# A two-layer hybrid transformer step: the odd layer's attention in the pool of the DeltaNet's preparation

## Chip, cores and metric

The kernel runs on one core of a Trainium2 chip. The metric is the device time of one execution in microseconds (us). Engines are named as the profile does: PE is TensorE (PEld its weight load, PEq, SPq and the like the sequencers that issue for an engine), DVE is VectorE, ACT is ScalarE, POOL is GpSimd, and SP is the engine that issues most DMAs. Each engine runs its own queue of instructions in order.

## What is computed

One step of a trunk with two layers on 128 context tokens and 1024 latent tokens, 1024 features wide. Each layer has a mixing part and a convolutional feed-forward part. The odd layer, which the change touches, mixes in two ways side by side: windowed attention with a sink (mixer C, 8 query heads and 2 key heads of 64) and a gated DeltaNet in two directions (mixer D). Cut to what matters, with jax.numpy as jnp:

```
cq, ck, cv, dq, dk, dv, da, db, dz = split_cols(h @ w_in, OD_SIZES)
q = axial_rope(cq...)            # latent tokens only; x1*cos - x2*sin, x1*sin + x2*cos
k = axial_rope(ck...)
# window_attn: 128 queries against their own block, both neighbours, and 128 cached keys
s_loc = jnp.where(valid, einsum(qn, kn) * scale, -inf)
s_ctx = einsum(qn, ck_cache) * scale
p = softmax_sink(concatenate([s_loc, s_ctx]), sink)
o_c = einsum(p, [vn, cv_cache])
# delta_scan, 64 tokens a chunk: a unit lower triangular system for each chunk and head
m_mat = a_mat + eye(64)
sol = triangular_solve(m_mat, rhs)
out = concatenate([o_c, o_d]) @ w_out
```

The 128 context tokens attend to each other without a window and without rotation. The gates dz (z0 to z3 below) multiply the DeltaNet's output much later.

## The kernel before

All matrices are float32. A projection splits weights and activations into a high and a low part and sums three matmuls for each block of 128 features (`gemm8`, L156 to L158: high by high, high by low, low by high). One chunk of weights is 128 x 1024: SP loads it (L134), ACT casts the high part `whi` (L141), DVE subtracts it to get the low part `wlo` (L144). One projected chunk of 128 columns takes 72 matmuls, in three blocks of tokens with 24 each.

`odd_1` (L1258) prepares the DeltaNet in pool "md". For four pairs of heads p = 0 to 3, `prep(p)` builds the matrices and `side(p)` the next pair's projections, and `inv(p)` inverts the 32 x 32 blocks of the systems on DVE: two directions with 31 steps of two instructions, a product `syst` (L1455) and a subtraction into `sysN` (L1457). POOL's queue stores the result in `n_dram` (L1460). `weave(main, fill)` and `mix` put steps of one generator between the steps of another. `side(3)` projects chunk c5 (values) and c4 (keys) of mixer C beside inv(2). Then `tail()` projects the query chunks c0 to c3, one for each pair of query heads. ACT copies each out (`df`, L1469) and makes a second copy with 32-row pieces swapped (L1473, four copies for each piece of tokens). `rope` (L1502) turns keys and queries: POOL or DVE multiplies the swapped copy by sines (L1506), DVE the other by cosines (L1507) and adds (L1509), and the result goes to `c_dram`. inv(3) is mixed into this on DVE. The order of DVE and POOL is written by hand there.

Then the pool closes and `odd_2` (L1535) runs in a new one, "mc": it projects the gates z0 and z3 (`odd_gate`), loads keys, values and queries from `c_dram` again (`cf`, `qp`), splits keys into `ks` and `kl` (L537 to L539) and queries into `qs` (L530, L531), and runs 36 attention units: for each pair p one unit with the 128 context queries (128 keys) and eight with 128 latent queries (512 keys inside, 384 at the ends). A unit's scores (PE L551, L552) go through the maximum `mx` (DVE L607), the negated maximum `nm` (L615), the exponential (ACT L617), the reciprocal of the sum and the normalisation (DVE L629, L632), the transposition `ptr` (PE L641, copied to `pt` by ACT L643) and the product with the values `pvo` (PE L652). `out` splits its result into `hh` (ACT L1622, then DVE L1623). `attn` has three units in flight: a turn issues the scores and the maximum of unit u, the normalisation of u-1, the transposition of u-2 and the product of u-3. The queries of the next pair are split in pieces of 576 columns during the units n = 2 and later of the current one.

As filler between units, `merge(p, d)` joins the inverted 32-blocks to 64-blocks: DVE transposes `tv` into `dT` (L1577), and for each third of the chunks PE does a group of small matmuls (a "quad", L1583, 24 records in the trace), ACT copies `zs` (L1589), PE does a second quad, and DVE writes the negated result into `tv` (L1597, two instructions): twelve quads for a pair of heads. `tv` is cleared by POOL first (L1568). The filler gets 1.8 units of debt for each attention unit. The orders of PE and DVE are written by hand here.

Of the kernel before, what the change touches and what calls it, by code (L numbers as in the profile page):

```python
# [9 lines left out]
F32 = mybir.dt.float32  # L10
# [43 lines left out]
class Net:  # L54
    def __init__(self, ctx, tc, I, O, dbg=None):
# [13 lines left out]
        self.nsc, self.sci = 6, 0  # L69
# [529 lines left out]
    def attn_exp(self, mp, u):  # L599
# [4 lines left out]
        for i in range(2):  # L604
            t = mp.tile([128, 512], F32, name="sc", tag=f"sc{self.sci}", bufs=1)
# [28 lines left out]
    def attn_tr(self, mp, u):  # L634
# [3 lines left out]
        for i in range(2):  # L638
            pt = self.pmt("ptr")
            for j in range(nk // 128):  # L640
                nc.tensor.transpose(pt[:, j * 128:(j + 1) * 128], u["sc"][i][:, j * 128:(j + 1) * 128], self.ident)  # L641
            t = mp.tile([128, 512], F32, name="pt", tag="pt", bufs=4)
            nc.scalar.copy(t[:, :nk], pt[:, :nk])  # L643
            u["pt"].append(t)
# [587 lines left out]
    def conv_ev(self, mp, w, dst):  # L1232
# [3 lines left out]
        def ev(b, ps):  # L1236
            n = FB[b][1]
            m = n - 2
            t = mp.tile([128, 388], F32, name="u", tag="du", bufs=2)
# [18 lines left out]
    def odd_1(self, mp, zp):  # L1258
        nc, I = self.nc, self.I
        mm = nc.tensor.matmul  # L1260
        D = self.dr
        self.kq_dram = D.tile([128, 18, 4, 4, 64], F32, name="kq_dram")
# [5 lines left out]
        dcw = mp.tile([128, 12, 3], F32, name="dcw", tag="dcw", bufs=1)  # L1268
        nc.sync.dma_start(dcw, I["dcw"])
        tri = {}  # L1270
        for nm in ("le", "ge", "gt", "lt", "bd"):
            tri[nm] = mp.tile([128, 128], F32, name=f"tri{nm}", tag=f"tri{nm}", bufs=1)
            nc.sync.dma_start(tri[nm], I[f"tri_{nm}"])
        half = []
        for d in range(2):
            t_ = tri["le" if d == 0 else "ge"]
            h = mp.tile([128, 64], F32, name="th", tag=f"th{d}", bufs=1)
            nc.vector.tensor_tensor(out=h, in0=t_[:, 0:64], in1=t_[:, 64:128], op=ALU.add)
            half.append(h.unsqueeze(1).to_broadcast([128, 18, 64]))
        g = mp.tile([128, 18, 8], F32, name="dg", tag="dg", bufs=1)  # L1280
# [4 lines left out]
        def gates():  # L1285
# [10 lines left out]
            sel = mp.tile([128, 18, 2, 8], F32, name="dsel", tag="dsel", bufs=1)  # L1296
# [7 lines left out]
            dtb = mp.tile([128, 8], F32, name="dtb", tag="dtb", bufs=1)  # L1304
            alg = mp.tile([128, 8], F32, name="alg", tag="alg", bufs=1)
# [5 lines left out]
            ab = mp.tile([128, 18, 8], F32, name="dabs", tag="dabs", bufs=1)  # L1311
# [20 lines left out]
        def df():  # L1332
            return mp.tile([128, T], F32, name="df", tag="df", bufs=4)
# [12 lines left out]

        def prep(p):
# [4 lines left out]
            for d in range(2):  # L1352
                X = mp.tile([128, 18, 64], F32, name="X", tag=f"am{d}", bufs=1)
                gg = g[:, :, 4 * d + p:4 * d + p + 1].to_broadcast([128, 18, 64])
                nc.vector.tensor_tensor(out=X, in0=gg, in1=half[d], op=ALU.mult)
                es.append((X, mp.tile([128, 18, 64], F32, name="E", tag=f"E{d}", bufs=1)))
            for x, nm in enumerate("kq"):
                s2[nm] = mp.tile([128, T], F32, name="s2", tag=f"aq{x}", bufs=1)
# [24 lines left out]
            def tok(nm, dr):  # L1383
                tt = mp.tile([128, T], F32, name="tt", tag="tt", bufs=2).rearrange("p (c t) -> p c t", t=64)
# [17 lines left out]
            aq = [mp.tile([128, 18, 64], F32, name="aq", tag=f"aq{d}", bufs=1) for d in range(2)]  # L1402
            am = [mp.tile([128, 18, 64], F32, name="am", tag=f"am{d}", bufs=1) for d in range(2)]
# [23 lines left out]
        def inv(p):  # L1427

            sy = []
            for d in range(2):  # L1430
                M = mp.tile([72, 32, 32], F32, name="sysM", tag=f"sysM{d}", bufs=1)
                N = mp.tile([72, 32, 32], F32, name="sysN", tag=f"sysN{d}", bufs=1)
# [8 lines left out]
                sy.append((M, N, tmp))  # L1441
            yield 0.0
            for jj in range(31):
                for d in range(2):
# [14 lines left out]
            for d in range(2):  # L1459
                nc.gpsimd.dma_start(self.n_dram[d, p], sy[d][1])  # L1460

        def proj_c(i):

            f = df()
# [11 lines left out]
            Q["c", i], Q["w", i] = f, w  # L1476

        def side(p):
# [6 lines left out]
            else:  # L1485
                yield from proj_c(5)
                nc.sync.dma_start(self.c_dram[5], Q["c", 5])
# [5 lines left out]
        self.plan += [("wi1", x) for x in (5, 4, 0, 1, 2, 3, 18, 21)]  # L1493
# [4 lines left out]
        cs, sn = Q["ropec"], Q["ropes"]  # L1498
# [3 lines left out]
        def rope(i):  # L1502
            f, w = Q["c", i], Q["w", i]
            r = f[:, 128:]
            eng = nc.gpsimd if i != 3 else nc.vector
            eng.tensor_tensor(out=w, in0=w, in1=sn, op=ALU.mult)  # L1506
            nc.vector.tensor_tensor(out=r, in0=r, in1=cs, op=ALU.mult)  # L1507
            yield
            nc.vector.tensor_tensor(out=r, in0=r, in1=w, op=ALU.add)  # L1509
            (nc.sync if i != 3 else nc.gpsimd).dma_start(self.c_dram[i], f)  # L1510
            yield

        def tail():
            prev = 4
            for i in range(4):
                pr, rp = proj_c(i), rope(prev)
                for c in pr:
                    next(rp, None)
                    yield c
                prev = i  # L1520
            for _ in rope(prev):
                pass

        E = mybir.EngineType
        with self.tc.manual_schedule(engines={E.DVE, E.Pool}):
            t, iv = tail(), inv(3)
            next(t)
            next(iv)
            for _ in range(2):
                next(t)  # L1530
            for _ in self.mix(t, iv, 1, 4):
                pass


    def odd_2(self, mp, zp):  # L1535
        nc, I = self.nc, self.I

        z0 = self.odd_gate(zp, 0)
        next(z0)
        mm = nc.tensor.matmul  # L1540
        R2 = [slice(0, 64), slice(64, 128)]
        kf = mp.tile([128, T], F32, name="cf", tag="cf", bufs=2)
        nc.sync.dma_start(kf, self.c_dram[4])
        vf = mp.tile([128, T], F32, name="cf", tag="cf", bufs=2)
        nc.sync.dma_start(vf, self.c_dram[5])
        mk = mp.tile([128, 1280], F32, name="maskC", tag="maskC", bufs=1)
        nc.sync.dma_start(mk, I["maskC"])
        VAR = [(0, 512), (512, 384), (896, 384)]
        sk = mp.tile([128, 4, 2], F32, name="sink", tag="sink", bufs=1)
        nsk = mp.tile([128, 4, 2], F32, name="nsink", tag="nsink", bufs=1)  # L1550
        nc.sync.dma_start(sk.rearrange("p a b -> p (a b)"), I["sink"].to_broadcast([128, 8]))
        nc.vector.tensor_scalar(out=nsk, in0=sk, scalar1=-1.0, scalar2=None, op0=ALU.mult)
        ks = [mp.tile([128, 1280], F32R, name="ks", tag=f"cks{i}", bufs=1) for i in range(2)]
        kl = self.new_kl(mp, "ckl", 1)
        ck = mp.tile([128, 128], F32, name="ck", tag="cck", bufs=1)
        nc.sync.dma_start(ck, I["ckT"])
        vt = mp.tile([128, 10, 128], F32, name="vt", tag="cvt", bufs=1)
        nc.sync.dma_start(vt[:, 8, :], I["cvc"])
        for _ in z0:
            pass  # L1560
        z3 = self.odd_gate(zp, 3)
        for _ in z3:
            pass

        def merge(p, d):

            t = self.tv[:, 2 * p + d]
            nc.gpsimd.memset(t, 0.0)  # L1568
            for r in range(2):
                for k in range(2):  # L1570
                    s0 = 64 * r + 32 * k
# [856 lines left out]
```

## Time and profile before

| | us |
|---|---|
| median of three runs | 3364.06 (3362.83 to 3365.55) |
| profiled execution | 3366.79 |
| its span | 3365.0 |
| PE busy in the span | 3209.0 (95%) |
| DVE busy | 2053.2 (61%) |
| ACT busy | 1432.6 (43%) |
| POOL busy | 659.9 (20%) |
| chain of work that ended last: PE, DVE, ACT | 82%, 9%, 4% |

Times of the trace count from the span's start. A busy share is an average over very different stages, so the rows below are taken from the stage that the change touches, 1951 to 2242 us. Busy time of PE is that of its matmuls, of which each is shown with its modelled end, so neighbouring ones overlap; starts are the better measure. The granted clock (PEclk) is a share of full speed.

### The profile page before, as it was taken

Reading aid. Unit: us, or ns where it says so; the run is one execution under the profiler, and the core shown is the slowest. Engines: PE = TensorE matmul, PEld = TensorE weight load, DVE = VectorE, ACT = ScalarE, POOL = GpSimd, SP = SyncE. Lnnn points to the kernel's source line nnn. Section 1 sums busy time; section 2 is a strip of 40 time slices with the busy share of each in tenths; the row PEclk is TensorE's granted clock in tenths of the full one; section 3 lists DMA queues with packets and bytes.
Section 4 is the critical chain, followed back from the end, with each engine's and each line's share of the span. In section 5 each row is a group of like instructions: output and inputs, shape, how many; then the busy total and the mean of one; then the engine's idle time right before and its main releaser. Section 6 shows DMA issues by size and latency. Waiting matters only on the chain.

```text
span 3365.0 us, 58552 instructions
## 1 busy us (share of the span) xinstructions
PE 3209.0 (95%) x23071; PEld 3042.3 (90%) x23071; DVE 2053.2 (61%) x4323; ACT 1432.6 (43%) x3264; POOL 659.9 (20%) x829
## 2 busy tenths in 40 slices
PE   7999999899999999999899977989989999999997
PEld 4999988789999999999799877878889999999997
DVE  5355677757554555555658887767675445444556
ACT  4465655536454444442554535640642222222223
POOL 1000011114554454450300131013220000000002
PEclk8999998999999999999899988999989999999999
DMA  5211233441222222221224444226301111111111
GB/s 205 83 55 57 80 100 108 131 165 62 90 79 80 79 86 79 83 88 45 81 78 131 108 123 137 63 111 190 121 13 43 44 40 44 40 43 44 39 44 69
DMA packets 183422, 282.73 MB, mean 84 GB/s; under 512 B 82518, under 2 KB 126294, under 8 KB 183020
## 3 DMA queue, kind: packets, MB, share of 16 engines
q1 hardware_dynamic: 153892, 233.84, 22.3%
q10 hardware_dynamic: 25176, 30.20, 2.9%
q0 software_dynamic: 4080, 14.94, 1.6%
q8 instruction: 183, 3.00, 0.4%
q14 instruction: 91, 0.75, 0.1%
HBM read 230.56 MB, written 48.37 MB: 83 GB/s over the span
## 4 chain that ended last, share of the span: by engine, by line
PE 82%; DVE 9%; ACT 4%; issue 2%; DMA 2%; POOL 1%; SPq 0%; DVEq 0%; POOLq 0%; ACTq 0%
PE g L156 16%; PE g L157 16%; PE g L158 16%; PE g L2125 5%; PE g L2123 5%; PE g L2124 5%; PE g L1960 4%; PE pvo L652 1%; PE kqs L1731 1%; PE ptr L641 1%; DVE sysN L1457 1%; DVE syst L1455 1%; PE s L551 1%; PE s L552 1%; PE g L1583 1%
## 5 line engine op out<-in xcount | busy, mean ns | idle before, releaser
L156 PE MATMUL g<-hh,whi 128*128 128x386 f32 (+2 forms) x3264 | 1123.4, 344 | 18.9 <-ACT df L1473 13.3
L158 PE MATMUL g<-hh,wlo 128*128 128x386 f32 (+2 forms) x3264 | 1110.2, 340 | 9.1 <-DVE wlo L144 8.9
L157 PE MATMUL g<-hl,whi 128*128 128x386 f32 (+2 forms) x3264 | 1114.6, 341 | 2.8 <-DVE hl L426 2.8
L156 PEld LDWEIGHTS g<-hh,whi 128*128 128x128 f32 x3264 | 621.3, 190 | 30.9 <-ACT df L1473 14.8
L158 PEld LDWEIGHTS g<-hh,wlo 128*128 128x128 f32 x3264 | 619.5, 190 | 11.2 <-DVE wlo L144 10.7
L157 PEld LDWEIGHTS g<-hl,whi 128*128 128x128 f32 x3264 | 620.4, 190 | 6.5 <-DVE hl L426 3.8
L2034 DVE SCALAR_TENSOR_TENSOR u<-g,cw,u 128x384 f32<-128x384 f32 (+1 forms) x264 | 163.2, 618 | 530.1 <-ACT u L2033 529.9
L2033 ACT ACTIVATE u<-g,cw 128x384 f32<-128x384 f32 (+1 forms) x264 | 153.9, 583 | 770.2 <-PE g L158 770.2
L518 DVE SCALAR_TENSOR_TENSOR x<-g,ada,x 128x128 f32<-128x128 f32 (+1 forms) x608 | 294.7, 513 | 203.2 <-PE g L2125 190.0
L141 ACT CAST whi<-wraw 128x1024 fp32r<-128x1024 f32 (+2 forms) x202 | 200.9, 995 | 443.1 <-PE g L2124 240.0
L2124 PE MATMUL g<-gl,whi 128*128 128x384 f32 (+1 forms) x1008 | 341.4, 339 | 1.9 <-DVE gl L2089 1.9
L2123 PE MATMUL g<-gh,whi 128*128 128x384 f32 (+1 forms) x1008 | 342.7, 340 | 0.2
L2125 PE MATMUL g<-gh,wlo 128*128 128x384 f32 (+1 forms) x1008 | 342.4, 340 | 0.0
L144 DVE TENSOR_TENSOR wlo<-wraw,whi 128x1024 fp32r<-128x1024 f32 (+2 forms) x214 | 256.8, 1201 | 95.0 <-ACT whi L141 94.8
L299 POOL TENSOR_TENSOR adat<-wada,adas 128x384 f32<-128x384 f32 x168 | 174.5, 1039 | 315.7 <-DMA wada<-in_adaw 287.6
L299 POOL TENSOR_TENSOR wada<-wada,adas 128x384 f32<-128x384 f32 x168 | 191.8, 1142 | 13.2
L2124 PEld LDWEIGHTS g<-gl,whi 128*128 128x128 f32 x1008 | 190.9, 189 | 2.4 <-issue 2.4
L2123 PEld LDWEIGHTS g<-gh,whi 128*128 128x128 f32 x1008 | 190.7, 189 | 0.8 <-issue 0.8
L2125 PEld LDWEIGHTS g<-gh,wlo 128*128 128x128 f32 x1008 | 189.9, 188 | 0.0
L2035 DVE SCALAR_TENSOR_TENSOR u<-g,cw,u 128x384 f32<-128x384 f32 (+1 forms) x264 | 163.4, 619 | 9.3
L2070 POOL MEMSET gh<- 128x1 f32 x44 | 4.3, 99 | 782.0 <-PE g L2125 777.8
L1960 PE MATMUL g<-hh,whi 128*128 128x384 f32 (+1 forms) x384 | 116.1, 367 | 11.4 <-DVE xr L518 7.2
(377 smaller groups left out, 4783.0 us busy)
## 6 DMA issues: line engine op xcount, KB each, us to landing
wraw<-in_ffnup SPq DMA_DIRECT2D x88, 512.0 KB
wraw<-in_wi SPq DMA_DIRECT2D x50, 512.0 KB
wada<-in_adaw ACTq DMA_DIRECT2D x112, 192.0 KB
wada<-in_adaw SPq DMA_DIRECT2D x80, 256.0 KB
kq<-kq_dram SPq DMA_DIRECT2D x36, 512.0 KB
wraw<-in_ffndn SPq DMA_DIRECT2D x40, 384.0 KB
wraw<-in_wo SPq DMA_DIRECT2D x16, 512.0 KB
wada<-in_adaw ACTq DMA_DIRECT2D x56, 128.0 KB
```

Of the source, the lines that this page charges most:

```text
L141: nc.scalar.copy(hi[:, :n], raw[:, :n])
L144: nc.vector.tensor_tensor(out=lo[:, c], in0=raw[:, c], in1=hi[:, c].bitcast(F32), op=ALU.subtract)
L156: mm(ps[:, :n], w, ah[:, k, c0:c0 + n], start=(k == 0), stop=False)
L157: mm(ps[:, :n], w, al[:, k, c0:c0 + n], start=False, stop=False)
L158: mm(ps[:, :n], lo[:, k * 128:(k + 1) * 128], ah[:, k, c0:c0 + n], start=False, stop=(k == 7))
L299: nc.gpsimd.tensor_tensor(out=d[:, :m], in0=w[:, :m], in1=sb[:, j, sl], op=ALU.mult)
L518: nc.vector.scalar_tensor_tensor(out=xr[:, t:t + nn], in0=ps[:, o:o + nn], scalar=gate[:, m, j:j + 1], in1=xr[:, t:t + nn], op0=ALU.mult, ...
L1960: mm(ps[:, :n], a[:, w], src[:, 2 * k + j, c0:c0 + n], start=(k + x == 0), stop=(k + x == 5))
L2035: nc.vector.scalar_tensor_tensor(out=t, in0=ps[:, 2:n], scalar=w[:, 2:3], in1=t, op0=ALU.mult, op1=ALU.add)
L2123: mm(ps[:, :n], hi[:, o:o + 128], gh[:, c0:c0 + n], start=(s == 0), stop=False)
L2124: mm(ps[:, :n], hi[:, o:o + 128], gl[:, c0:c0 + n], start=False, stop=False)
L2125: mm(ps[:, :n], lo[:, o:o + 128], gh[:, c0:c0 + n], start=False, stop=(s == ng - 1))
```

## The change

- `odd_2` runs inside `odd_1`'s pool, with tags shared between tiles of both (`pack`, `five`, `ring`). Keys, values and queries stay in the chip's memory: `c_dram` isn't written or read.
- Only c0 and c1 are projected ahead of the attention. c2, z0, z3 and c3, twelve blocks of 24 matmuls, are filler between the first attention units, which now get 2.8 of debt each.
- inv(3) is done one direction after the other (`behind`), four steps of it ahead of a unit of latent queries; the merges start behind it, and so stand in the units of p = 2 and 3 and behind the last unit.
- The swapped copy is made by four SP loads of 32 x 1024 inside the chip's memory (`rope`, L1495 in the changed kernel) instead of by ACT; all three operations of a rotation are on DVE.
- Queries are split for one unit at a time (`head`: two casts on ACT, two subtractions of 64 x 128 on DVE).
- The outputs of p = 0 and 1 are copied by ACT to `oT` and split later in wide operations (`late`); those of p = 2 and 3 are split as before.

The core of the diff:

```diff
@@ inv
-        def inv(p):
+        def inv(p, ds=(0, 1)):
...
@@ proj_c, rope
-            w = df()[:, :TS] if i < 5 else None
...
-                    if w is not None and t0 >= TP:
-                        for a in range(4):
-                            c = (a ^ 1) * 32
-                            nc.scalar.copy(w[32 * a:32 * a + 32, t0 - TP:t0 - TP + n], ps[c:c + 32, o:o + n])
...
+        def rope(i):
+
+            f = Q["c", i]
+            w = df(2 if i == 4 else 1)[:, :TS]
+            for a in range(4):
+                c = (a ^ 1) * 32
+                nc.sync.dma_start(w[32 * a:32 * a + 32], f[c:c + 32, TP:])
+            r = f[:, TP:]
+            yield
+            nc.vector.tensor_tensor(out=r, in0=r, in1=Q["ropec"], op=ALU.mult)
+            yield
+            nc.vector.tensor_tensor(out=w, in0=w, in1=Q["ropes"], op=ALU.mult)
+            yield
+            nc.vector.tensor_tensor(out=r, in0=r, in1=w, op=ALU.add)
+            yield
...
@@ odd_2
+        def head(q, c0):
+
+            t = []
+            for i in range(2):
+                qs = mp.tile([128, 128], F32R, name="qs", tag=f"cqs{i}", bufs=2)
+                self.stack_q(q, lambda ap: ap[:, c0:c0 + 128], i, qs, lambda ap: ap)
+                t.append(qs)
+            return t
...
+                if p < 2:
+                    ev = lambda t0, oT=oTs[p]: lambda o: nc.scalar.copy(oT[:, t0:t0 + 128], o[:, :128])
...
+                    if n > 1 and late and p > 1:
+                        late.pop(0)()
+                    next(back, None)
+                    yield dict(q=head(q, 128 + n * 128), ks=ks, kl=kl,
...
+        def behind():
+
+            for d in range(2):
+                it = inv(3, (d,))
+                while True:
+                    for _ in range(4):
+                        if next(it, None) is None:
+                            break
...
+        def projections():
+            yield from turned(chunk(2), rope(1))
+            yield from self.odd_gate(zp, 0)
+            yield from self.odd_gate(zp, 3)
+            yield from turned(chunk(3), rope(2))
...
         def fill():
             yield from self.hq
-            yield 6.6
+            for _ in rope(3):
+                yield 2.0
             self.tv = self.hpool.tile([128, 8, 18, 64], F32, name="tv", tag="hl")
+            for _ in back:
+                pass
+            load(0)
             for p in range(4):
-                yield from self.mix(merge(p, 0), merge(p, 1), 1, 1)
+                for x, c in enumerate(self.mix(merge(p, 0), merge(p, 1), 1, 1)):
+                    if x == 10 and p < 3:
+                        load(p + 1)
+                    yield c
...
+            self.weave(self.attn(mp, units(), 2.8, 2), fill())
```

What stands on DVE ahead of the first scores. In the kernel before, the rows run from the end of inv(3) to the first maximum; `L1506` to `L1509` are the rotation of c3, `kl` and `qs` the splits of keys and queries:

```order
L1506 TENSOR_TENSOR df<-df,rope 128x1024
L1507 TENSOR_TENSOR df<-df,rope 128x1024
L1509 TENSOR_TENSOR df<-df 128x1024
L144 TENSOR_TENSOR wlo<-wraw,whi 128x1024
L1552 TENSOR_SCALAR nsink<-sink 128x8
L539 TENSOR_TENSOR kl<-ck,ks 64x128 x2
L539 TENSOR_TENSOR kl<-cf,ks 64x128 x2
L531 TENSOR_TENSOR qs<-qp,qs 64x128 x2
L607 ISA sc,mx<-s,maskC 128x128
```

In the changed kernel they run from the last instruction of inv(2); `L1498` to `L1502` are the rotation of c0:

```order
L1473 TENSOR_TENSOR sysN<-sysN,syst 72x31
L540 TENSOR_TENSOR kl<-df,ks 64x128
L540 TENSOR_TENSOR kl<-df,ks 64x512 x4
L145 TENSOR_TENSOR wlo<-wraw,whi 128x1024
L1498 TENSOR_TENSOR df<-df,rope 128x1024
L1500 TENSOR_TENSOR df<-df,rope 128x1024
L1502 TENSOR_TENSOR df<-df 128x1024
L532 TENSOR_TENSOR qs<-df,qs 64x128 x2
L608 ISA ring,mx<-s,maskC 128x128
```

All of inv(3) and three of the four query rotations now come behind the first maximum; the projections c2, c3, z0 and z3 do so on PE.

DVE among the first units of 512 keys, from one normalisation to the next unit's maximum (`L607`, after it `L608`). Before:

```order
L632 TENSOR_SCALAR sc<-sc,ri 128x512 x2
L1623 TENSOR_TENSOR hh<-pvo,hh 128x128
L1597 TENSOR_SCALAR tv<-g 32x6x32 x2
L531 TENSOR_TENSOR qs<-cf,qs 64x576
L607 ISA sc,mx<-s,maskC 128x512
L607 ISA mx 128x1
```

After (eight instructions are the inversion's four steps):

```order
L633 TENSOR_SCALAR ring<-ring,ri 128x512 x2
L1471 TENSOR_TENSOR syst<-sysM,sysN 72x240
L1473 TENSOR_TENSOR sysN<-sysN,syst 72x20x12
L1471 TENSOR_TENSOR syst<-sysM,sysN 72x247
L1473 TENSOR_TENSOR sysN<-sysN,syst 72x19x13
L1471 TENSOR_TENSOR syst<-sysM,sysN 72x252
L1473 TENSOR_TENSOR sysN<-sysN,syst 72x18x14
L1471 TENSOR_TENSOR syst<-sysM,sysN 72x255
L1473 TENSOR_TENSOR sysN<-sysN,syst 72x17x15
L532 TENSOR_TENSOR qs<-df,qs 64x128 x2
L608 ISA ring,mx<-s,maskC 128x512
L608 ISA mx 128x1
```

The queries that stand just ahead of a maximum are now those of the same unit, behind the inversion; before, they were a piece of the next pair's.

PE around the end of one unit's scores, where `ptr` and `pvo` belong to units two and three earlier. Before, with two merge quads behind them and the next unit's scores:

```order
L551 MATMUL s<-ks,qs 128x128
L552 MATMUL s<-kl,qs 128x128
L641 MATMUL ptr<-ident,sc 128x128 x8
L652 MATMUL pvo<-pt,vt 64x128 x6
L1583 MATMUL g<-dT,am 64x64 x24
L551 MATMUL s<-ks,qs 128x384
L552 MATMUL s<-kl,qs 128x384
```

After, with the first three of 24 matmuls of a projection, behind which the next unit's scores stand:

```order
L552 MATMUL s<-ks,qs 128x128
L553 MATMUL s<-kl,qs 128x128
L642 MATMUL ptr<-ident,ring 128x128 x8
L657 MATMUL pvo<-ring,vt 64x128 x8
L157 MATMUL g<-hh,whi 128x384
L158 MATMUL g<-hl,whi 128x384
L159 MATMUL g<-hh,wlo 128x384
```

The quads in these first units have moved to later units, and a block of a projection has taken their place in twelve of the first 19 turns.

## Rows read from the trace of the kernel before

**Rows 1.** Stretches: length, busy time and instructions of each engine, clock, DMA.

```profile
core 0: us, PE busy (x) PEld busy (x) DVE busy (x) ACT busy (x) POOL busy (x), PEclk, DMA share, GB/s
1955.00:1963.00 8.00, 8.00 (x47) 8.00 (x47) 8.00 (x28) 3.94 (x11) 5.95 (x1) 1.00 0.70 250
1951.00:2069.00 118.00, 86.94 (x440) 83.39 (x437) 92.45 (x249) 44.27 (x98) 35.83 (x28) 0.83 0.44 141
2069.00:2242.00 173.00, 154.02 (x2172) 137.44 (x2173) 130.82 (x402) 115.08 (x333) 18.27 (x77) 0.91 0.22 54
```

**Rows 2.** PE's waits, 1951 to 2069: total us, times, longest.

```profile
PE g L156 <- ACT df L1473: 13.3, 4, 7.0
PE g L158 <- DVE wlo L144: 8.9, 2, 6.7
```

**Rows 3.** Single instructions: start, us, engine, line, operation, tiles, idle time before.

```profile
1957.05 11.09 POOL L1506 TENSOR_TENSOR df<-df,rope 128x1024 f32<-128x1024 f32 x1 [3.47 <-DVE syst L1455]
...
1965.87 2.56 DVE L1457 TENSOR_TENSOR sysN<-sysN,syst 72x256 f32<-72x256 f32 x1
...
1977.74 0.69 PE L158 MATMUL g<-hh,wlo 128*128 128x386 f32 x1 [6.70 <-DVE wlo L144]
...
2069.16 0.45 PE L551 MATMUL s<-ks,qs 128*128 128x128 f32 x1 [5.34 <-POOL tv L1568]
```

**Rows 4.** DVE's groups, 1951 to 2069: count, busy us, mean ns, idle before.

```profile
L1457 DVE TENSOR_TENSOR sysN<-sysN,syst 72x255 f32<-72x255 f32 (+15 forms) x108 | 39.6, 377 | 2.3
L1455 DVE TENSOR_TENSOR syst<-sysM,sysN 72x87 f32<-72x87 f32 (+15 forms) x107 | 36.6, 353 | 8.0 <-DMA sysM<-am_dram 5.4 <-POOL df L1506 2.5
L144 DVE TENSOR_TENSOR wlo<-wraw,whi 128x1024 fp32r<-128x1024 f32 x6 | 7.3, 1213 | 1.9 <-ACT whi L141 1.9
```

**Rows 5.** PE's waits, 2069 to 2251: total us, times, longest.

```profile
PE g L1583 <- DVE dT L1577: 17.1, 4, 4.9
```

**Rows 6.** DVE's waits, 2069 to 2242: total us, times, longest.

```profile
DVE hh L1623 <- ACT hh L1622: 27.1, 27, 2.6
```

**Rows 7.** PE's single instructions around one unit of 512 keys.

```profile
2092.05 1.61 PE L1583 MATMUL g<-dT,am 64*64 64x64 f32 x48
2093.59 0.44 PE L551 MATMUL s<-ks,qs 128*128 128x384 f32 x1
...
2094.21 0.39 PE L551 MATMUL s<-ks,qs 128*128 128x384 f32 x1
...
2096.80 0.39 PE L1583 MATMUL g<-tv,zs 64*64 64x64 f32 x6
```

**Rows 8.** DVE's groups by shape, 2069 to 2242.

```profile
L607 DVE CUSTOM_DVE_ANT_0 sc<-s,maskC 128x512 f32<-128x512 f32 x48 | 31.3, 688 | 3.6 <-PE s L552 3.0
...
L1597 DVE TENSOR_SCALAR tv<-g 32x192 f32<-32x192 f32 x48 | 16.9, 352 | 2.2 <-PE g L1583 1.4
L1577 DVE STREAM_TRANSPOSE dT<-tv 128x1152 f32<-128x1152 f32 x8 | 10.5, 1352 | 0.0
L1623 DVE TENSOR_TENSOR hh<-pvo,hh 128x128 fp32r<-128x128 f32 x36 | 10.4, 289 | 27.1 <-ACT hh L1622 27.1
L531 DVE TENSOR_TENSOR qs<-cf,qs 64x576 fp32r<-64x576 f32 x12 | 9.0, 752 | 1.2 <-ACT qs L530 1.0
...
L607 DVE CUSTOM_DVE_ANT_0 sc<-s,maskC 128x128 f32<-128x128 f32 x8 | 2.2, 290 | 1.8 <-PE s L552 1.5
...
L531 DVE TENSOR_TENSOR qs<-qp,qs 64x128 fp32r<-64x128 f32 x2 | 0.6, 286 | 0.3 <-ACT qs L530 0.3
```

**Rows 9.** DVE's single instructions, one unit's first maximum and what follows its normalisation.

```profile
2129.51 0.69 DVE L607 CUSTOM_DVE_ANT_0 sc<-s,maskC 128x512 f32<-128x512 f32 x1
...
2131.95 0.28 DVE L1623 TENSOR_TENSOR hh<-pvo,hh 128x128 fp32r<-128x128 f32 x1
```

**Rows 10.** Two more stretches, columns as in rows 1.

```profile
2155.40:2161.70 6.30, 6.24 (x54) 5.47 (x56) 2.86 (x10) 2.54 (x8) 0.39 (x2) 0.50 0.01 3
2204.05:2210.00 5.95, 5.95 (x117) 5.37 (x118) 3.87 (x16) 4.32 (x17) 0.79 (x4) 1.00 0.01 3
```

More of the change, by code (lines that the diff above doesn't have):

```diff
@@ L1497, in odd_1, with odd_2, five @@
             self.weave(prep(p), side(p))
-        cs, sn = Q["ropec"], Q["ropes"]
         nc.sync.dma_start(self.O["ncv"], Q["c", 5][:, 0:128])
         nc.sync.dma_start(self.O["nck"], Q["c", 4][:, 0:128])
[L1502 to L1535, printed above, removed]
+        self.odd_2(mp, zp, Q, proj_c, rope, inv)
+    def odd_2(self, mp, zp, Q, proj_c, rope, inv):
         nc, I = self.nc, self.I
-        z0 = self.odd_gate(zp, 0)
-        next(z0)
         mm = nc.tensor.matmul
         R2 = [slice(0, 64), slice(64, 128)]
[L1542 to L1547, printed above, removed]
         VAR = [(0, 512), (512, 384), (896, 384)]
+        def five(name, tag, dt=F32):
+            return mp.tile([128, 1280], dt, name=name, tag=tag, bufs=1)
         sk = mp.tile([128, 4, 2], F32, name="sink", tag="sink", bufs=1)
@@ L1551, in odd_2 @@
         nc.sync.dma_start(sk.rearrange("p a b -> p (a b)"), I["sink"].to_broadcast([128, 8]))
[L1552 to L1557, printed above, removed]
@@ new lines, in chunk, with turned @@
+        def chunk(i):
+            pr = proj_c(i)
+            for c in pr:
+                yield c
+            qr[i] = Q["c", i]
+        def turned(g, r):
+            for c in g:
+                next(r, None)
+                yield c
+            for _ in r:
+                pass
+        def projections():
[3 more added lines that the diff above has]
+            yield from turned(chunk(3), rope(2))
@@ L1688, in odd_2 @@
         E = mybir.EngineType
         with self.tc.manual_schedule(engines={E.PE, E.DVE}):
-            self.weave(main(), fill())
+            nc.vector.tensor_scalar(out=nsk, in0=sk, scalar1=-1.0, scalar2=None, op0=ALU.mult)
+            k4 = rope(4)
+            next(k4)
+            c0 = chunk(0)
+            next(c0)
+            for _ in k4:
+                pass
+            ks = [five("ks", f"am{i}", F32R) for i in range(2)]
+            kl = [five("kl", f"E{i}", F32R) for i in range(2)]
@@ new lines, in odd_2 @@
+            for i in range(2):
+                o = 64 * (1 - i)
+                nc.gpsimd.memset(kl[i][o:o + 64].bitcast(F32), 0.0)
+            next(c0)
+            keys()
+            vt = mp.tile([128, 10, 128], F32, name="vt", tag="aq0", bufs=1)
+            mk = five("maskC", "aq1")
+            nc.sync.dma_start(mk, I["maskC"])
+            for _ in c0:
+                pass
+            values()
+            oTs = [mp.tile([128, T], F32, name="oT", tag=f"tt{x}", bufs=1) for x in range(2)]
@@ new lines, in odd_2, with ring @@
+            for _ in turned(chunk(1), rope(0)):
+                pass
+            back = behind()
+            self.hq = projections()
+            self.scr = self.ring(mp, ("sysM1", "sysN1", "scx"), 1024)
+            self.ptr = self.ring(mp, ("du0", "du1"), 512) + self.ring(mp, ("pack",), 1024)
+            self.weave(self.attn(mp, units(), 2.8, 2), fill())
+            self.scr = self.ptr = None
+    def ring(self, mp, tags, n):
+        t = [mp.tile([128, n], F32, name="ring", tag=g, bufs=1) for g in tags]
+        return [a[:, c:c + 512] for a in t for c in range(0, n, 512)]
```

187 lines of the change are left out of this document (89 added, 98 removed).

## Prediction

> **What bounds the kernel now.** I read the table of stretches first, then what each engine waited for in two of them, then the groups of VectorE's work, then single instructions.
>
> The change touches the odd layer between 1951 us (the last DeltaNet preparation is done) and 2242 us (the last attention output is split). In the first stretch, up to 2069, PE is busy 86.94 of 118.00 us; in the second, the 36 attention units, 154.02 of 173.00 [rows 1]. At full speed its 432 matmuls need 73 us, at 0.170 each: 47 start in 8.00 us [rows 1]. PE waits there for the copies of the swapped queries (13.3 us), for the low halves of the weights (8.9) [rows 2] and, before the first score, 5.34 for a memset [rows 3]. VectorE is busy 92.45 us in it, mostly inverting blocks: 108 and 107 instructions, 39.6 and 36.6 us [rows 4].
>
> In the second stretch PE is busy 89% of the time, and its largest waits are four, 17.1 us, for the transposed blocks dT [rows 5]. VectorE has 130.82 us, and 27.1 of its idle time stands before the split of an output, hh, which waits for ScalarE's copy [rows 6]. So PE is nearly the bound here, with VectorE behind it. A unit of 512 keys takes PE 3.21 us (scores at 2093.59, the next work at 2096.80), a pair of merge quads 1.54 (2092.05 to 2093.59) [rows 7]. All 36 units take 173/36 = 4.8 us each with the quads.
>
> **The change, part by part.**
>
> *First scores, earlier.* Projections c2, c3, z0 and z3 leave the first stretch, the queries are not stored and reloaded, and ScalarE no longer makes the swapped copies. Nothing moves ahead of the low half of c1's weights on VectorE; it runs behind inv(2), so PE's 6.70 us wait for it [rows 3] stays, but for what the 11.09 us operation on POOL at 1957.05 did to VectorE beside it: one instruction in 2.56 us, where 0.38 is the mean, 2.2 us [rows 3, 4]. That weight half, done at 1977.7 before, when PE's wait ends, is then done at 1975.5. From there VectorE decides, in the order shown: key rotation 3 x 1.21 = 3.6 (its operations have the size of the low half's, 1.213), the last 17 instructions of inv(2) at 0.365 = 6.2, eight subtractions for kl (four at 0.286, four of half a weight chunk at 0.6) = 3.5, c2's low half 1.2, query rotation 3.6, the first split 0.6 [rows 4, 8]. Together 18.7: the first scores at **1994** instead of 2069.16 [rows 3], 75 us earlier. PE has c1 done by 1989 meanwhile (66 of its 72 matmuls left at 1975.5, 11.2 us, and some 2 for a slow start). The rotation's swap is now four loads on SP's queue, behind the last use of c4's tile; the trace does not show them. Bounds: 0 if they land beside c2's low half, and 5.4, which is what VectorE waited for loads of sysM [rows 4]. I take 0 because two operations stand between. The 1994 lies in 1992 to 2000.
>
> *What moves into the attention.* Twelve blocks of 24 matmuls (4.1 us each at 0.170, 49 us of PE); all of inv(3), 62 x (0.377 + 0.353) = 45.3 us of VectorE; nine rotation operations, 10.9; four low halves, 4.9. VectorE gains query splits unit by unit, 72 x 0.286 = 20.6 for 12 x 0.75 = 9.0, and loses 18 splits of outputs (5.2), given back as four wide ones (3.0) [rows 4, 8].
>
> *A loop that was not there.* Before, a whole pair's queries were split a few units ahead. Now qs of a unit stands on VectorE behind all that the last unit and the inversion want there, PE's scores wait for it, and VectorE's maximum waits for the scores. Queued behind that wait are the normalisation, the inversion's steps, and the next qs. One turn costs qs 0.57, the first half of the scores 0.66 (0.62 by 2093.59 to 2094.21, and a little for the signal), and 2.44 from the first maximum to the end of the normalisation (2129.51 to 2131.95) [rows 7, 8, 9]: 3.67.
>
> Units 0 to 18 (merges have not begun): 19 x 3.67 = 69.7; three units with 128 keys save 2 x 0.4 each, 2.4; inversion 45.3, rotations 10.9, low halves 4.9: 128.4. A turn with four inversion steps takes 3.67 + 2.9 = 6.6; a turn with a gemm block takes PE 3.21 + 4.1 = 7.3, so some of the twelve run over VectorE's turn. I add 2: **130 us**.
>
> Units 19 to 35 (merges): 17 x 3.67 = 62.4 less 0.8; sixteen hh at 0.29, each behind 1.0 us of waiting for ScalarE as now (27.1 over 27) [rows 6, 8]; 36 tv at 0.352, six dT at 1.352, the wide splits 3.0: 61.6 + 20.6 + 12.7 + 8.1 + 3.0 = **106 us**. PE has 17 x 3.21 and 36 quads at 0.77, 82 us, and sits below. So the saving is eaten twice: the projections' 49 us cost nothing on PE, but VectorE's turn is longer than PE's was.
>
> Behind the last scores: 2.44, two dT 2.7, twelve quads 9.2 and some 2 for the copies between them, **16 us**; before, the quads ended with the units. What follows loads x from memory; the quads may hide some of that, or not. I take nothing.
>
> Sum: 1994 + 130 + 106 + 16 = 2246, against 2242: +4 us on a run of 3366.79, whose median is 3364.06. **Forecast 3368 us.**
>
> *The clock.* PE waited for dT four times, 4.3 us on average [rows 5]. [...] The changed loop leaves PE idle 6.6 - 3.2 = 3.4 us in the seven of the first 19 turns that hold no block. I count nothing, because a PE at half rate still has slack against VectorE in these turns, and the idle time is below those of the rows. [...]
>
> **The rivals.**
>
> *VectorE runs ahead and PE is the bound (faster).* If qs is done while PE is still in its block or its quads, scores follow without a wait. PE's work is then 154.02 + 49 = 203 us, the end 1994 + 203 = 2197 with no idle time, or 2216 with the 19 us of idle time that this stretch has now [rows 1]: 3319 to 3338. VectorE's own work, 130.8 + 45.3 + 10.9 + 4.9 + 11.6 + 3.0 - 5.2 = 201 us, would just allow it. It decides if the mean turn is under 6.0 us instead of the 6.6 of my sums (236/36). For it: neither engine alone needs more than 203 us, and in this stretch VectorE now idles 42 us. Against it: qs is last in the turn's order, and where both engines have equal work, each wait in the loop is lost.
>
> [...]
>
> *The change does not give its head start (slower).* If the swap loads stand behind weight loads in SP's queue, and c4's tile comes free late, first scores come at 2004 or later (two waits of 5.4): +14, 3378.
>
> **How the numbers follow.** The forecast, the loop with 3.67 us per turn, has 0.58 and its own range 3354 to 3384 (turns 0.3 us shorter or longer on 36). PE as the bound 0.24, half clock 0.13, no head start 0.05. A measurement of this kernel tells 0.2%, 6.7 us, from no change. Of the forecast's 0.58, 0.06 is faster than that, 0.30 within it, 0.22 slower; with the rivals: faster 0.30, same 0.30, slower 0.40. The range for 8 in 10 reaches into the first rival to 3328, which leaves out about 0.12 of its lower part, and above to 3394, which leaves out 0.06.
>
> **What would show it.** First scores near 1994 show the head start. VectorE's waits for PE's scores some 0.6 us in each of 36 units, and PE's for qs, show the loop; if PE waits little for qs, the first rival holds. The first merge quads should start near 2124, the last output 2240 to 2250. [...] I am wrong if VectorE's instructions overlap more than in the 2.44 us, if ScalarE's casts of queries come late behind its exponentials and lengthen each turn, or if the next stage starts on other grounds than the end of the merges.

## The result and the profile after

The changed kernel takes **3394.41 us** (median of 4 runs, 3393.54 to 3395.66) beside 3364.81 (3362.83 to 3368.6) for the kernel before: ratio 1.0094 (95% interval 1.0081 to 1.0107). It is slower by 29.6 us, where 3368.0 was forecast and 3394 was the upper end of the range. Its profiled execution took 3394.28, with a span of 3392.5.

It is in the stage that the change touches. The stretches (columns as in [rows 1]) are cut here at the first score, at the first score of unit 19, and at the end of the last merge quad:

```profile
core 0: us, PE busy (x) PEld busy (x) DVE busy (x) ACT busy (x) POOL busy (x), PEclk, DMA share, GB/s
1951.00:1996.00 45.00, 28.98 (x157) 27.32 (x155) 38.68 (x112) 15.21 (x35) 9.27 (x11) 0.84 0.65 196
1996.00:2138.00 142.00, 111.71 (x758) 103.42 (x758) 110.06 (x325) 69.27 (x208) 19.93 (x52) 0.88 0.18 48
2138.00:2272.00 134.00, 103.61 (x1680) 92.69 (x1682) 82.98 (x249) 68.06 (x198) 7.17 (x35) 0.90 0.20 48
```

Where PE was busy 89% of the attention stretch before [rows 1], it is now busy 79% and 77%, and DVE 78% and 62%: neither engine is full. What each waits for, 1990 to 2275 (total us, times, longest), answers to [rows 5, 6]; PE's waits come first:

```profile
PE s L552 <- DVE qs L532: 50.0, 27, 7.0
PE s L552 <- ACT qs L531: 7.8, 1, 7.8
```

```profile
DVE ring L608 <- PE s L553: 38.4, 42, 4.8
DVE hh L1602 <- ACT hh L1601: 26.1, 18, 2.2
DVE tv L1585 <- PE g L1571: 9.7, 10, 2.6
DVE df L1498 <- DMA df<-df: 5.7, 1, 5.7
```

In the kernel before, over the same window:

```profile
PE s L551 <- DVE qs L531: 0.7, 1, 0.7
DVE sc L607 <- PE s L552: 6.9, 8, 1.7
```

PE's scores wait 50 us for the split queries, where they waited 0.7 before, and DVE's maximum waits 38 us for those scores, where it waited 6.9. Each engine waits for the other in turn.

The head start came nearly as forecast. Single instructions of DVE and PE (start, us, engine, line, operation, tiles, idle time before), answering to the first score in [rows 3]:

```profile
1992.26 1.23 DVE L1498 TENSOR_TENSOR df<-df,rope 128x1024 f32<-128x1024 f32 x1 [5.66 <-DMA df<-df]
...
1996.34 0.45 PE L552 MATMUL s<-ks,qs 128*128 128x128 f32 x1 [7.79 <-ACT qs L531]
```

The first score stands at 1996.34 instead of 2069.16, although DVE waited 5.66 us for the loads that swap the rows. Behind the stage PE waits for `x` in both kernels, until 2250.57 before and until 2281.65 now. So 73 us of head start have become 31 us of delay, of which 3.6 are made up later (the two profiled executions differ by 27.5). Before, then after:

```profile
2250.57 0.91 PE L1960 MATMUL g<-hh,whi 128*128 128x386 f32 x2 [3.88 <-DVE x L518]
...
2281.65 0.79 PE L2006 MATMUL g<-hh,whi 128*128 128x386 f32 x2 [2.83 <-DVE x L519]
```

Two turns show how; turn u here runs from the first score of unit u to that of unit u+1. In the first, turn 9, no inversion step stands in the turn, and a block of a projection does. DVE:

```profile
2066.60 0.75 DVE L633 TENSOR_SCALAR ring<-ring,ri 128x384 f32<-128x384 f32 x2
2067.36 0.60 DVE L532 TENSOR_TENSOR qs<-df,qs 64x128 fp32r<-64x128 f32 x2
2072.72 0.56 DVE L608 CUSTOM_DVE_ANT_0 ring<-s,maskC 128x384 f32<-128x384 f32 x1 [4.76 <-PE s L553]
```

PE in the same turn, first and last matmul of the block, and the scores:

```profile
2067.81 0.44 PE L157 MATMUL g<-hh,whi 128*128 128x384 f32 x1
...
2071.93 0.34 PE L159 MATMUL g<-hh,wlo 128*128 128x384 f32 x1
2072.11 0.28 PE L552 MATMUL s<-ks,qs 128*128 128x256 f32 x1
```

The queries were ready at 2067.96, but PE's scores stand behind the block and start at 2072.11. DVE has nothing left in this turn and is idle for 4.76 us. In the second, turn 22, the merges run. DVE, and behind it PE:

```profile
2163.02 0.90 DVE L633 TENSOR_SCALAR ring<-ring,ri 128x512 f32<-128x512 f32 x2
2165.34 0.29 DVE L1602 TENSOR_TENSOR hh<-pvo,hh 128x128 fp32r<-128x128 f32 x1 [1.41 <-ACT hh L1601]
2165.54 1.45 DVE L1585 TENSOR_SCALAR tv<-g 32x192 f32<-32x192 f32 x4
2167.00 0.60 DVE L532 TENSOR_TENSOR qs<-df,qs 64x128 fp32r<-64x128 f32 x2
2168.23 0.69 DVE L608 CUSTOM_DVE_ANT_0 ring<-s,maskC 128x512 f32<-128x512 f32 x1 [0.62 <-PE s L553]
```

```profile
2162.77 0.88 PE L657 MATMUL pvo<-ring,vt 128*64 128x128 f32 x12
2163.58 1.61 PE L1571 MATMUL g<-tv,zs 64*64 64x64 f32 x48
2167.44 0.41 PE L552 MATMUL s<-ks,qs 128*128 128x384 f32 x1 [2.24 <-DVE qs L532]
```

Here it is PE that has run out of work. The queries stand on DVE behind the split of an output, `hh`, which waits for ACT's copy of PE's `pvo` of the same turn. That product is done at 2163.65, but the copy starts only at 2165.06, because it stands on ACT behind the exponentials of unit 22, of which the second runs from 2164.26 to 2164.97:

```profile
2163.54 0.72 ACT L618 ACTIVATE ring<-ring,nm 128x512 f32<-128x512 f32 x1
...
2165.06 0.24 ACT L1601 CAST hh<-pvo 128x128 fp32r<-128x128 f32 x1
```

So the chain of this turn runs PE scores, DVE maximum, ACT exponentials, ACT copy, DVE `hh`, DVE `tv` and `qs`, and PE scores again.

### The profile page after: what moved, and what is told of

Same layout as the page of the kernel before. It is cut to its first block, busy times and chain, and to the rows that moved or that the text cites. A ratio compares the mean times of both kernels' runs of the same rounds, so it can differ in the third digit from the quotient of the medians.

```text
span 3392.5 us, 58657 instructions
## 1 busy us (share of the span) xinstructions
PE 3212.0 (95%) x23071; PEld 3044.8 (90%) x23071; DVE 2068.8 (61%) x4367; ACT 1419.9 (42%) x3262; POOL 642.1 (19%) x824
## 4 chain that ended last, share of the span: by engine, by line
PE 82%; DVE 10%; ACT 4%; issue 2%; DMA 1%; POOL 1%; SPq 0%; DVEq 0%; ACTq 0%; POOLq 0%
PE g L157 16%; PE g L158 16%; PE g L159 16%; PE g L2171 5%; PE g L2169 5%; PE g L2170 5%; PE g L2006 4%; PE ptr L642 1%; PE pvo L657 1%; PE kqs L1777 1%; PE s L552 1%; PE s L553 1%; DVE sysN L1473 1%; DVE syst L1471 1%; PE att L1143 1%
## 5 line engine op out<-in xcount | busy, mean ns | idle before, releaser
L300 POOL TENSOR_TENSOR adat<-wada,adas 128x384 f32<-128x384 f32 x168 | 172.1, 1024 | 316.8 <-DMA wada<-in_adaw 286.9
L552 PE MATMUL s<-ks,qs 128*128 128x128 f32 (+2 forms) x256 | 77.7, 317 | 57.8 <-DVE qs L532 50.0
```

Of the source, the lines that this page charges most:

```text
L300: nc.gpsimd.tensor_tensor(out=d[:, :m], in0=w[:, :m], in1=sb[:, j, sl], op=ALU.mult)
```

## The experiments

Three theories of the extra time stood against each other. **Loop**: the queries of a unit are split on DVE behind instructions that wait for PE and ACT, and PE's scores wait for them. **Work**: DVE simply has too much to do in the attention. **Clock**: the low clock that PE is granted behind its waits (0.50 in turn 17, behind one of 6.98 us) lengthens the blocks and with them the turns. Waits named below are those of 1985 to 2290 unless said otherwise; ratios are to the kernel before, run beside.

**1. Queries one unit ahead.** The split of unit u+1 is issued before the inversion steps and the maximum of unit u. The tile keeps its two buffers, and the work on every engine stays the same.

```diff
+            nxt = hd(0)
+            for j, (p, n) in enumerate(seq):
...
+                cur, nxt = nxt, (hd(j + 1) if j < 35 else None)
...
-                    yield dict(q=head(q, 128 + n * 128), ks=ks, kl=kl,
+                yield dict(q=cur, ks=ks, kl=kl,
```

> The changed kernel with one edit: VectorE splits the queries of unit u+1 ahead of the inversion steps and the maximum of unit u, so that PE's scores no longer wait for the end of VectorE's turn. Nothing else moves. Theory L (the loop of query split, scores and maximum costs the time): PE's 50 us of waits for the split, 27 of them, fall under 12 us, VectorE's 38 us of waits for scores halve, the attention ends near 2245 instead of 2272, and the kernel takes 3362 to 3372 us. Theory C (PE's half clock behind its waits costs it): the same direction, but only because the waits go; not told apart here. Theory W (VectorE has too much work in this stretch, the order is indifferent): 3389 to 3396 us, since its work is the same.

3357.15 us (3352.38 to 3363.89), ratio 0.9973 (0.9964 to 0.9982): 37 us less than the changed kernel, and a little under the kernel before. PE's wait for DVE's queries is gone (its largest are now 9.3 us for the normalisation and 9.3 for ACT's first cast), and two of DVE's three largest waits in the attention shrink with it, from 26.1 and 38.4 to 15.1 and 10.2:

```profile
DVE hh L1602 <- ACT hh L1601: 15.1, 15, 2.1
DVE tv L1585 <- PE g L1571: 10.5, 9, 3.0
DVE ring L608 <- PE s L553: 10.2, 8, 4.5
```

The last quad ends at 2234.83 instead of 2272.26, 37.4 us earlier, which is the whole gain. With the same instructions, the work theory cannot explain it. The granted clock rises as well, from 0.88 to 0.91 in the stretch 1996 to 2138, so this experiment alone does not part the loop from the clock; experiments 6 and 7 do.

**2. Output cast on VectorE.** Both halves of `hh` on DVE, so that it does not wait for ACT.

```diff
-            nc.scalar.copy(hi, o[:, :128])
+            nc.vector.tensor_copy(hi, o[:, :128])
```

> The changed kernel with one edit: the high half of an output of pairs 2 and 3 is cast by VectorE itself, ahead of its subtraction, instead of by ScalarE, behind whose exponentials it stands. VectorE gets 18 more casts of about 0.3 us and loses its waits for ScalarE there (26.1 us over 18). Theory L: each of these 18 turns is shorter by 1.45 - 0.3, some 1.1 us, together 18 to 21 us: 3374 to 3378 us. Theory W: VectorE's work grows by 5 us: 3394 to 3400 us. Theory C: some microseconds less, 3385 to 3392 us, from shorter waits of PE.

3382.27 us (3373.7 to 3388.85), ratio 1.0048 (1.0032 to 1.0064): 12 us less than the changed kernel, where 18 to 21 were expected. It shortens the loop, which stays: PE still waits 42.7 us for queries.

**3. PE kept busy.** Twenty matmuls whose result is not used, in each of the seven turns without a block.

```diff
+        if warm is not None and u is not None and warm.pop(0):
+            w = self.pgt()
+            for x in range(20):
+                nc.tensor.matmul(w[:, :384], u["ks"][0][:, 0:128], u["ks"][0][:, 128:512], start=(x == 0), stop=(x == 19))
```

> The changed kernel with 20 more matmuls of 128x384 (3.5 us at full clock, their result is not used) in each of the seven turns among units 0 to 18 that hold no projection block, so that PE isn't idle there before the next scores. The loop is left as it is. Theory C (half clock costs a good part of the loss): granted clock of 1994 to 2138 rises from 0.88 to over 0.97 and the kernel gains 8 to 15 us: 3379 to 3386 us. Theory L (VectorE's turns set the time, PE at half clock has slack): within 4 us of 3394, since the extra matmuls fill idle time and the few scores at half clock cost 0.5 us a turn.

3399.97 us (3398.58 to 3402.18), ratio 1.0102 (1.0087 to 1.0117). The granted clock did rise, from 0.88 to 0.94 in the same stretch, and the time rose by 5.6 us, which neither theory expected:

```profile
1996.00:2138.00 142.00, 127.65 (x860) 119.27 (x861) 106.76 (x313) 67.29 (x200) 19.71 (x50) 0.94 0.16 43
```

This does not price the clock by itself, because the added matmuls take PE's time too. Turns 3, 7, 10 and 17, which got them, are together 6.0 us longer, and the first score, ahead of them all, stands 1.8 us later. Turns 4, 8, 15 and 21, granted 0.60 to 0.83 in the changed kernel and 1.00 here, are together 5.1 us shorter. Turn 8, in the changed kernel and in this run:

```profile
2056.80:2065.40 8.60, 8.60 (x53) 8.00 (x53) 4.11 (x12) 3.31 (x10) 1.83 (x5) 0.81 0.51 131
2060.30:2067.30 7.00, 7.00 (x53) 6.63 (x53) 3.88 (x11) 3.22 (x10) 1.43 (x4) 1.00 0.57 152
```

So the low clock did lengthen a few turns of the changed kernel, but the blocks did not run at half rate: eleven of the twelve took 4.1 to 4.2 us from first start to last, and only the first, in a turn granted 0.62, took 6.3. The four turns behind PE's longest waits for queries (3.90 to 6.98 us) were granted 0.50 to 0.83, but 24 of the 35 turns 0.95 or more.

**4. tv cleared by ScalarE.** ACT copies a zero instead of POOL's memset.

```diff
-                nc.gpsimd.memset(t, 0.0)
+                nc.scalar.copy(t, zero.unsqueeze(1).to_broadcast([128, 18, 64]))
```

> The changed kernel with one edit: the eight blocks of tv are cleared by ScalarE copying zeros instead of by POOL's memsets. In the changed kernel VectorE's normalisation of two times 128x512 beside these memsets took 3.48 us instead of 0.90. If POOL's memsets slow VectorE there, this pair takes 0.9 again, the turn of unit 16 (10.15 us) falls by 2 to 3 us, and the kernel takes 3389 to 3393 us, ScalarE's eight copies being some 1.2 us each beside its waits. If the 3.48 us had another cause, the pair stays at 3.5 and the time within 2 us of 3394.

3391.38 us (3387.33 to 3395.23), ratio 1.0076 (1.006 to 1.0091): 3 us less, a difference that the times alone do not tell from none. The trace shows what it is. In the changed kernel the memsets fell on a normalisation; POOL, then DVE:

```profile
2116.88 2.06 POOL L1554 MEMSET tv<- 128x1152 f32 x2
...
2119.21 3.32 POOL L1554 MEMSET tv<- 128x1152 f32 x3
```

```profile
2118.06 3.48 DVE L633 TENSOR_SCALAR ring<-ring,ri 128x512 f32<-128x512 f32 x2
```

and without them the same two instructions take 0.90:

```profile
2116.22 0.90 DVE L633 TENSOR_SCALAR ring<-ring,ri 128x512 f32<-128x512 f32 x2
```

Turn 16 went from 10.15 to 7.58 us, 2.6 less.

**5. Edits 1, 2 and 4 together.**

> The changed kernel with the three edits together: queries split one unit ahead, the outputs' high halves cast by VectorE, tv cleared by ScalarE. Alone they gave 3357.2, 3382.3 and 3391.4 us where the changed kernel has 3394.4. Theory L: the first removes the loop, and in it 15.1 us of VectorE's waits for ScalarE's casts are left, of which the second takes perhaps half; with 3 us of the third the kernel takes 3344 to 3353 us, below both kernels. If with the loop gone PE and not VectorE sets the turns, the other two edits give nothing: 3354 to 3359 us.

3357.85 us (3351.85 to 3361.86, 11 runs), ratio 0.9981 (0.9972 to 0.999), the same as with edit 1 alone; the 3344 to 3353 of the loop theory was missed. The cast that was worth 12 us in the loop adds nothing to the time once the loop is cut. In the profiled executions the last quad ends 3.9 us earlier than in experiment 1 (2230.97 and 2234.83) and the times are equal (3359.45 and 3359.42); what takes the 3.9 us back stands behind this stage and stays open.

**6. The kernel before, with its queries split for one unit at a time.** One part of the change alone: pairs 1 to 3 take `head` instead of pieces of 576 columns for the next pair.

```diff
-                    yield dict(q=[q[i][:, 128 + n * 128:256 + n * 128] for i in range(2)], ks=ks, kl=kl,
+                    yield dict(q=hq(128 + n * 128), ks=ks, kl=kl,
```

> The kernel before with one part of the change alone: the queries of pairs 1 to 3 are split for one unit at a time, just ahead of that unit's scores on VectorE, instead of a pair ahead in pieces of 576 columns; the tile for the split queries has one buffer instead of two. Nothing else of the change is in it. Theory L: VectorE's work grows by 54 x 0.29 - 9.0 = 6.7 us, and 27 turns get 0.66 us of waiting for their own scores each, 18 us, of which some is hidden behind waits that are there now; with PE's 17.1 us of waits for dT partly overlapped, the attention grows by 15 to 30 us and the kernel takes 3380 to 3396 us. Theory W (order indifferent, only the work counts): 3365 to 3373 us.

3403.5 us (3400.47 to 3407.09), ratio 1.0119 (1.0105 to 1.0133): 39 us lost by this one part, more than the change as a whole loses, and more than I expected. PE's largest wait and DVE's two largest, 2069 to 2290:

```profile
PE s L551 <- DVE qs L531: 35.4, 23, 2.5
```

```profile
DVE hh L1631 <- ACT hh L1630: 49.0, 34, 2.6
DVE sc L607 <- PE s L552: 19.4, 32, 1.7
```

The wait for ACT's copy, 27.1 us before [rows 6], is 49.0: it stands in the loop and grows with it.

**7. The same kernel, split one unit ahead.** As 6, with the split of the next unit issued before the maximum, as in 1.

> The kernel before with the per-unit split of queries of the earlier run (3403.5 us), but each split placed one unit ahead, in front of the maximum of the unit before its own. The same small instructions, the same number, only their place differs. Theory L (the place makes the loop): PE's 35.4 us of waits for the split fall under 5, and the kernel takes 3364 to 3374 us, the 6.7 us of more work on VectorE being partly hidden. If it were the number of small operations on VectorE and ScalarE that cost 39 us, it would stay at 3395 to 3404 us.

3367.73 us (3363.49 to 3374.26), ratio 1.0004 (0.9994 to 1.0013). The waits, same window, are those of the kernel before again; PE waits 0.7 us once for queries:

```profile
PE s L551 <- DVE qs L531: 0.7, 1, 0.7
```

```profile
DVE hh L1631 <- ACT hh L1630: 27.4, 27, 2.1
DVE sc L607 <- PE s L552: 4.8, 8, 1.7
```

The clock does not explain the difference. Units 19 to 24 were granted 1.00 in both kernels and hold nearly the same work of PE, and took 34.8 us in experiment 6 and 24.8 here (columns as in [rows 1]):

```profile
2174.90:2209.70 34.80, 24.35 (x379) 21.68 (x379) 22.45 (x77) 20.81 (x64) 2.33 (x12) 1.00 0.12 36
2163.40:2188.20 24.80, 24.11 (x380) 21.55 (x378) 20.59 (x72) 19.17 (x59) 2.15 (x11) 1.00 0.15 50
```

54 small subtractions in place of 12 wide ones cost nothing that can be measured; their place cost 39 us.

**8. Inversion and nine blocks ahead of the attention.** Changed kernel, with inv(3), c2, z0 and z3 done before the first unit, and c3 in units 11 to 13.

> The changed kernel with the inversion of the last pair and the projections c2, z0 and z3 (nine of the twelve blocks) put ahead of the first scores, beside each other as in the kernel before; c3 stays between units 11 to 13, the merges begin with unit 18 as before, and the query loop is left as it is. First scores near 2042 instead of 1996, since VectorE has 45 us of inversion and 6 us more ahead of them; units 0 to 18 then take 19 x 3.67 and 13 us of other work, some 82 us instead of 142, and the rest is unchanged. Theory L (a moved step costs its own length and stretches turns that it shares with a block): stage ends 12 to 18 us earlier than in the changed kernel, 3376 to 3383 us. Theory W (VectorE's total work sets the end): 3391 to 3397 us.

3405.23 us (3397.66 to 3406.55), ratio 1.0119 (1.0105 to 1.0133); neither expectation was met, and the kernel is 11 us slower than the changed one. The profiled execution, 3397.66, is far below the median, so only the shape is read from it: first score at 2048.98 (52.6 later than in the changed kernel), units 0 to 18 in 91.2 us (50.6 less), last quad's end at 2273.04 (0.8 later). What left the attention came back ahead of it, so the stage ends no earlier; where the rest of the 11 us arises stays open. The run did measure the loop by itself, in turns that hold neither inversion nor block (PE's scores, DVE's queries released them):

```profile
2071.63 0.41 PE L552 MATMUL s<-ks,qs 128*128 128x384 f32 x1 [0.48 <-DVE qs L532]
...
2075.39 0.41 PE L552 MATMUL s<-ks,qs 128*128 128x384 f32 x1 [0.51 <-DVE qs L532]
...
2079.16 0.41 PE L552 MATMUL s<-ks,qs 128*128 128x384 f32 x1 [0.50 <-DVE qs L532]
```

Two turns of 3.76 and 3.77 us: my sum was 3.67.

**9. Edits 1 and 4, and a tile of its own for the first swap.** The four loads for c0 no longer wait for the tile that c4's rotation used; they go to the tile of a later output, which is taken up behind this rotation instead of ahead of it.

```diff
-            w = df(2 if i == 4 else 1)[:, :TS]
+            w = (df(2 if i == 4 else 1) if i else mp.tile([128, T], F32, name="w0", tag="tt0", bufs=1))[:, :TS]
```

> The changed kernel with the queries split one unit ahead, tv cleared by ScalarE, and the swapped copy for the first query rotation in a tile of its own (that of a later output), so that its four loads need not wait for the last use of c4's tile. In the changed kernel VectorE waited 5.66 us for these loads at 1992. If the tile was what held them, the first scores come near 1991 instead of 1997 and the kernel takes 3347 to 3354 us; if the loads stand behind weight loads on SP's queue or take that long themselves, 3354 to 3359 us, as with the splits ahead alone (3357).

3345.52 us (3342.97 to 3348.87), ratio 0.9941 (0.9929 to 0.9954): faster than both kernels, by 20 us than the kernel before. DVE's wait for the swap loads is gone, and the first score stands at 1989.96. Beside experiment 1, which lacks edit 4 and this tile, 11.6 us are gained. The first score is 7.3 us earlier (1997.23 there), and turn 17, where the memsets fell on a normalisation in experiment 1, takes 6.04 us instead of 9.73; the last quad ends at 2224.45 instead of 2234.83. With the loop cut too, a turn is long at a low clock now and then: in experiment 5 turn 4 was granted 0.72 and took 12.17 us, of which 0.9 was a wait for DVE's maximum, and here, at 1.00, it takes 8.47. The stretches, cut as above:

```profile
1990.00:2106.00 116.00, 104.96 (x758) 97.33 (x758) 102.87 (x315) 71.17 (x205) 13.03 (x43) 0.95 0.21 58
2106.00:2224.00 118.00, 98.64 (x1676) 89.05 (x1675) 86.15 (x257) 72.18 (x208) 7.45 (x36) 0.92 0.24 60
```

**10. The kernel before, with its output cast on VectorE.** Edit 2 on the other kernel.

> The kernel before with the high half of the outputs cast by VectorE instead of ScalarE. VectorE waited 27.1 us there for ScalarE in 27 of 36 units. Theory L says that waits count where VectorE's turn sets the time; before the change PE was busy 89% of this stretch and VectorE 76%, so most of them are slack: 3358 to 3366 us. If they count in full, 27 - 36 x 0.3 = 16 us go: 3346 to 3352 us.

3352.41 us (3345.39 to 3358.11), ratio 0.9963 (0.9951 to 0.9975), 13.6 us less. The loop theory missed here: it took these waits for mostly slack (3358 to 3366 us), and the time is nearer to the 3346 to 3352 that were expected if they count in full. So most of the wait of [rows 6] was on the path of the kernel before too, without a loop through the queries: PE's wait for `x` behind the stage ends at 2239.47 instead of 2250.57.

## Why the prediction was wrong in size and right in kind

The chain of the sum was: first scores 1994, units 0 to 18 in 130, units 19 to 35 in 106, 16 behind them, end 2246. Measured: 1996.34, 141.8 (unit 19 starts at 2138.17), 111.8 (unit 35 at 2250.01), 22.3 to the last quad's end, 2272.26. The 26 us that are missing are 2.3, 11.8, 5.8 and 6.3.

- **The loop, right.** It was named, with its place and its parts; the bare turn is 3.76 (experiment 8) where 3.67 was worked out, and experiments 1, 6 and 7 show that it is the cause. Two signs for it that the prediction gave came true: PE's waits for qs (27), and DVE's for scores, 0.62 to 0.63 where nothing else delays them. The two that name times missed with the sum: the first merge quad starts at 2142.62 instead of near 2124, and the last output is split at 2268.81 instead of 2240 to 2250.
- **First scores, right but for one term.** I took the swap loads at 0 and put 5.4 as the upper bound; DVE waited 5.66. Part of it was made up elsewhere, so that the score came 2.3 late.
- **Units 0 to 18: the step that failed is "I add 2".** The sum had DVE wait 19 x 0.66 = 12.5 us for scores, and 2 for blocks that outlast DVE's turn. Measured, 1996 to 2138:

```profile
DVE ring L608 <- PE s L553: 25.7, 21, 4.8
```

  That is 11.2 us more than 12.5 + 2. By my own numbers a turn with a block (7.3) is 0.7 above one with four inversion steps (6.6), and a turn without these steps, as turns 8 and 9, lies far below its block. I averaged DVE's work over the 19 turns and compared the mean. In a loop each turn lasts at least as long as the longer of the two engines in that turn, so the mean is only a floor; turn 12 lasted 7.96 us with PE busy for 6.7 and DVE for 6.9. Part of the 11.2 is the clock, which I put at nothing because a PE at half rate, as in the 0.50 of [rows 10], would still have slack: 2.2 us in the first block and 3.5 in turns 4, 8 and 15, an estimate from the rows of experiment 3. The memsets on POOL add 2.6 (experiment 4), which I did not price; other terms were 2.0 too large.
- **Units 19 to 35 and what follows: two waits mis-sized.** Sixteen hh at 1.0 us of waiting were taken from [rows 6]; there were 18 at 1.45 (26.1), 10 us more. The mean of before was measured where the loop did not exist; in the loop, 14 of the 18 copies start 0.3 to 1.7 us after the end of their `pvo`, right behind the exponentials of the same turn, as in turn 22, and these follow the late scores. The waits of tv for PE were taken as none and came to 9.7. Together 19.8, against 12.1 that these two stretches ran over; the other 7.7 are terms of mine that were too large, which the runs do not tell apart. That I could cost hh as work plus a fixed wait was the error of kind here: experiments 6 (49.0 us of it) and 1 (15.1) show that its size depends on whether the loop is closed.
- **The end of the stage, right.** I took nothing more for what follows. PE's wait for `x` ends 9.4 us after the last quad now, and before it ended 8.7 us after the last output (2241.84).
- **Rival: PE as the bound (0.24).** It did not hold: PE waited 50 us for queries. Even with the loop cut (experiment 1) the last quad ends at 2234.83, above the 2216 of that rival. One place where time is lost is turns 17 to 19 of that run, which hold inversion steps and rotations but no block: PE is busy there for 14.8 of 26.5 us. The rest is not told apart.
- **Rival: half clock in the loop (0.13).** It did not hold. No run shows a half clock that comes back behind every turn without a block: seven of the first 19 turns hold none, and the blocks in the four turns that follow such a turn (4, 8, 11 and 15, granted 0.81 to 1.00) took 4.1 to 4.2 us, like all but the first, 6.3. The granted clock of 1994 to 2124 is 0.89. What the clock did cost, some 7 us, is an estimate: 2.2 in the first block and 5.1 in turns 4, 8, 15 and 21 (experiment 3).
- **Rival: no head start (0.05).** The 5.66 us are one of its two waits.

What the change is worth without the loop can be read from experiment 1: 9 us less than the kernel before, and 20 less with experiment 9. The 73 us of head start went mostly, as far as the rows show, into the same work done later, since PE and DVE were already busy 89% and 76% of the stretch that received it [rows 1].

## What to carry to other kernels

When a small step feeds another engine each turn (a split, a cast, a load), issue it one turn ahead, in front of the instructions that wait for that engine; the same step behind them closes a loop, and here that was worth 37 us in one kernel and 39 in the other. When two engines exchange results each turn, compare their work turn by turn and take the longer one as the least that a turn can last, not the sums over the stage. A wait that stands in such a loop is no constant: the mean from the trace without the loop was 1.0 us here, and 1.45 came.

## What was not expected of the hardware

Memsets on POOL of 128x1152 floats slowed two TENSOR_SCALAR of DVE on 128x512 floats in the chip's memory from 0.90 to 3.48 us; with the clearing on ACT the pair took 0.90 again (experiment 4). DVE's pair took nearly four times as long, while the eight memsets took 1.05 to 1.33 us each, with a median of 1.06, beside 1.05 to 1.08 in the kernel before.

Four copies of 32 x 1024 floats inside the chip's memory, issued behind the last use of their tile, kept DVE waiting for 5.66 us; with a tile that was free earlier, DVE did not wait for them, and the first score came at 1989.96 instead of 1997.23 (experiments 9 and 1).
